# Block 0 of a decoder trunk: query, key, gate and pool columns by seven block products, with the memory's values folded into their weights afterwards

## The chip, the core and the metric

The kernel runs on one core of a Trainium2 chip. The metric is the time on the device for one launch, in microseconds (us). The engines of the core work side by side and wait for each other on semaphores: PE (TensorE) multiplies, ACT (ScalarE) and DVE (VectorE) work on rows of 128 partitions, POOL (GpSimd) here mostly issues DMAs, and SP (SyncE) issues most of the others. DMA moves data between the device memory and the core's own memory.

## What is computed

The reference is one layer of a decoder for 2048 tokens of width 1024, with a memory of 256 tokens, all in fp32. Cut to what matters here:

```python
def reference(x, mem, positions, ...):
    mem_n = rmsnorm(mem, mem_norm_g)
    h = rmsnorm(x, mix_norm_g)
    q, k, v, g, u = split(h @ w_in)            # five column groups of 512
    y_ret  = silu(g) * head_rmsnorm(retention(q, k, v, positions))   # rotary on q and k, 4 heads
    y_pool = pool_mixer(u, pool_w, pool_scale)                       # windows 2, 4, 8, 16
    x = x + concat(y_ret, y_pool) @ w_out
    x = x + cross_attn(rmsnorm(x, xa_norm_g), mem_n, wq, wkv, wo)    # 4 heads of 256
    x = x + conv_glu_ffn(rmsnorm(x, ffn_norm_g), w_up, conv_w, conv_b, w_down)
    return rmsnorm(x, final_norm_g)
```

## The kernel before

**Arithmetic.** Every fp32 operand of a large product is split into a high and a low part (`split`, L254: ACT writes the high part, DVE the low one), and a product is three matmuls that accumulate in one PSUM bank: high by high, high by low, low by high (`passes`, lines L269 to L271). A unit of 128 output columns by 512 tokens over the depth of 1024 is 8 depth tiles by 3, so 24 matmuls of 512 columns. PSUM has five banks for such units (`mm`) and three for small work (`aux`).

**Blocks.** The 2048 tokens are worked in two blocks of 1024. Block 0 runs through the projections, the retention and pooling heads, the output projection and the cross attention; then block 1 does the same; the feed-forward part and the last norm come behind both.

**Seven products.** Block 1 multiplies in the way of Strassen and Winograd. The 16 column groups of 128 of query, key, gate and pool are taken as eight pairs (`PAIRS`, L34). A pair, with the two halves of the depth and the two halves of the tokens, is a two by two block matrix, and its product needs seven block products in place of eight; each is 12 matmuls of 512 columns. For that, sums of quarters of the tokens are made on ACT and DVE (`quarter_sums`, L1603), sums of quarters of the weights by DMAs that add, issued on POOL, into the device tensor `Ad` (`weight_sums`, L1012), and products are added up in SBUF by `head_projections` (L1639). That function also applies the norm and the rotary tables, and starts `retention` (L784) for each head when its parts are there. The feed-forward part uses the same scheme.

**Block 0 before.** Block 0 uses eight products. `head_inputs` (L750) makes gate, query and key of one head as three groups of 48 matmuls, and `pool_group` (L690) the pool columns. The retention of the head before runs between the matmuls as a generator (`behind`), stepped as units go by.

**Folding.** The keys and values of the memory are known before any token arrives, so products of weights that only meet the memory are made once. `folded_weights` (L423) projects keys and values (`project`, 16 steps n of 24 matmuls of 256 columns each), folds the keys into the query weights (M, kept in the device tensor `Md`, 192 matmuls of 256 columns), the values into the output weights of the attention (VW, `VWd`, 96 matmuls of 512 columns), and the pool weights into the output projection (WP, `WPd`, 24 of 512 columns). It is a generator too. The main loop steps it with `folded(n)`: the 16 projection steps stand alone ahead of block 0, and M, VW and WP are taken in small portions between the groups of `head_inputs`. The list `per` says after which group how many portions come.

**Norms.** The squares of the block's tokens are made from the transposed tokens `xT`: ACT squares a tile (`squares_wide` and `load_x`), DVE adds tiles up, and PE sums over the partitions by small matmuls with a column of ones (`stats`), and spreads the factor over the partitions by matmuls with a matrix of ones (`spread`).

**Order.** Instructions of one engine run in the order in which the scheduler puts them, which mostly is the order of the code. A few are pinned (`keep_in_program_order`, `issue_after`). Loads go through SP's queue in order, results are stored through ACT's queue, and the sums of weights go through POOL's software queue; `under` is the generator of the sums, paced by `spacing` and `paced`. Raw weights have five places of 128x1024 in SBUF (`R`, `S`), pairs of split weights three (`Q`); the arenas `B`, `Z` and `TT` hold the rest.

## Time and profile before

| | us |
|---|---|
| runs shown | 2429.25, 2429.44, 2431.54 |
| median | 2429.44 |
| the profiled execution's own time (its span, first to last instruction) | 2429.8 |
| PE busy | 2412.5 (99%) |
| DVE busy | 1722.6 (71%) |
| ACT busy | 1292.3 (53%) |
| POOL busy | 306.1 (13%) |

The profile is of one execution, whose span is 0.36 us above the median. Matmuls overlap each other, so the mean duration of one in a group (some 390 ns) is no price. The price is the distance from start to start, which a full stretch of the view of windows gives as its length by its count. The same holds in a lesser degree for ACT, where a stretch of instructions with no gap between them gives the price of one.

By the trace, the K and V projections of the memory and the loading of block 0 take the first 60 us, with the M, VW and WP portions following among block 0's groups; the stores of VW are issued at 237 to 271 us. POOL's first round of weight sums is issued at 318.9 us. Block 1's values begin at some 650 us and its projections by seven products run to some 960 us.

### The profile page before, as it was taken

How to read it: one execution, taken by the hardware profiler on the slowest of the kernel's cores; microseconds unless marked ns; L12 is line 12 of the kernel's file. 1: busy time of each engine (PE TensorE's matmuls, PEld its weight loads, DVE VectorE, ACT ScalarE, POOL GpSimd, SP SyncE). 2: the span in 40 equal slices, each digit the busy share in tenths (PEclk: the TensorE clock that was granted, in tenths of full speed). 3: DMA queues.
4: the chain of work that ended last, by engine and by line, in shares of the span. 5: the costliest groups of instructions: out<-in, count | busy, mean ns of one | idle time of the engine just before them, and what ended most of it. 6: DMA issues, size and time to landing. Idle time of an engine off the chain costs nothing.

```text
span 2429.8 us, 33360 instructions
## 1 busy us (share of the span) xinstructions
PE 2412.5 (99%) x11328; PEld 2018.4 (83%) x11328; DVE 1722.6 (71%) x2911; ACT 1292.3 (53%) x2360; POOL 306.1 (13%) x477
## 2 busy tenths in 40 slices
PE   9999999999999999999999999999999999999998
PEld 8888888888888888888888888888888888888887
DVE  7756566655857775565788776887677698867875
ACT  6434423444545553334655555765555577666663
POOL 0000012154032444300001010020000000000000
PEclk9999999999999999999999999999999999999999
DMA  7233548699678899985568564755556479758951
GB/s 283 76 105 115 163 137 225 189 237 329 203 206 216 197 254 305 258 293 168 173 223 272 170 204 143 249 191 164 173 158 211 126 244 311 238 183 279 348 178 73
DMA packets 263627, 502.35 MB, mean 207 GB/s; under 512 B 28832, under 2 KB 58016, under 8 KB 263456
## 3 DMA queue, kind: packets, MB, share of 16 engines
q1 hardware_dynamic: 201424, 385.78, 48.3%
q0 software_dynamic: 37376, 86.00, 15.3%
q10 hardware_dynamic: 24656, 28.43, 3.4%
q8 instruction: 89, 1.46, 0.2%
q14 instruction: 82, 0.67, 0.1%
HBM read 398.65 MB, written 187.43 MB: 241 GB/s over the span
## 4 chain that ended last, share of the span: by engine, by line
PE 98%; DVE 1%; ACT 1%; DMA 0%; issue 0%; SPq 0%; DVEq 0%; ACTq 0%
PE mm L269 31%; PE mm L271 30%; PE mm L270 30%; PE aux L269 1%; PE aux L270 1%; PE aux L271 1%; PE aux L832 1%; PE aux L816 1%; PE aux L957 1%; PE aux L805 1%; PE aux L834 1%; DVE Z L241 0%; PE aux L350 0%; PE aux L807 0%; DMA R<-wkv 0%; PE aux L857 0%
## 5 line engine op out<-in xcount | busy, mean ns | idle before, releaser
L269 PE MATMUL mm<-G,Q 128*128 128x512 f32 (+1 forms) x1703 | 656.1, 386 | 3.8 <-ACT Q L257 2.5
L271 PE MATMUL mm<-G,Q 128*128 128x512 f32 (+1 forms) x1703 | 652.9, 384 | 1.4 <-DVE Q L241 1.4
L270 PE MATMUL mm<-G,Q 128*128 128x512 f32 (+1 forms) x1575 | 605.2, 384 | 0.4 <-DVE G L249 0.3
L270 PE MATMUL mm<-G,E 128*128 128x512 f32 x1084 | 421.5, 389 | 0.0
L269 PE MATMUL mm<-G,E 128*128 128x512 f32 x1084 | 420.0, 389 | 0.0
L271 PE MATMUL mm<-G,E 128*128 128x512 f32 x1084 | 419.3, 389 | 0.0
L269 PEld LDWEIGHTS mm<-G,Q 128*128 128x128 f32 x1703 | 320.1, 188 | 67.6 <-ACT Q L257 3.4
L271 PEld LDWEIGHTS mm<-G,Q 128*128 128x128 f32 x1703 | 320.1, 188 | 64.5 <-DVE Q L241 2.0
L270 PEld LDWEIGHTS mm<-G,Q 128*128 128x128 f32 x1575 | 296.0, 188 | 57.3 <-DVE G L249 0.8
L241 DVE TENSOR_TENSOR Z<-Z,mm 128x512 f32<-128x512 f32 (+1 forms) x310 | 207.6, 674 | 121.5 <-PE mm L271 115.7
L249 DVE SCALAR_TENSOR_TENSOR Z<-Z,vecs 128x1024 f32<-128x1024 f32 x176 | 224.8, 1281 | 50.2 <-ACT Z L1191 47.9
L271 PEld LDWEIGHTS mm<-G,E 128*128 128x128 f32 x1084 | 203.5, 188 | 42.4
L270 PEld LDWEIGHTS mm<-G,E 128*128 128x128 f32 x1084 | 203.6, 188 | 42.2
L269 PEld LDWEIGHTS mm<-G,E 128*128 128x128 f32 x1084 | 203.5, 188 | 42.1
L1128 ACT ACTIVATE E<-R 128x512 fp32r<-128x512 f32 (+1 forms) x165 | 101.4, 615 | 144.2 <-PE mm L270 138.3
L241 DVE TENSOR_TENSOR Q<-R,Q 128x512 fp32r<-128x512 f32 x158 | 108.1, 688 | 73.2 <-ACT Q L257 56.0
L241 DVE TENSOR_TENSOR T<-T 128x512 f32<-128x512 f32 (+3 forms) x202 | 138.6, 690 | 21.1 <-ACT T L416 12.1
L241 DVE TENSOR_TENSOR G<-T,G 128x512 fp32r<-128x512 f32 (+1 forms) x185 | 121.6, 677 | 26.5 <-ACT G L1075 13.5
L1075 ACT ACTIVATE G<-T 128x512 fp32r<-128x512 f32 x186 | 112.0, 623 | 32.4 <-DMA T<-Gd 25.7
L1191 ACT ACTIVATE Z<-Z,vecs 128x1024 f32<-128x1024 f32 x88 | 109.1, 1241 | 31.2 <-DVE Z L241 30.2
L1128 ACT ACTIVATE E<-S 128x512 fp32r<-128x512 f32 (+1 forms) x107 | 65.9, 616 | 108.6 <-PE mm L270 106.5
L241 DVE TENSOR_TENSOR E<-R,E 128x512 fp32r<-128x512 f32 (+1 forms) x129 | 86.6, 673 | 44.6 <-ACT E L1128 42.7
(356 smaller groups left out, 3838.2 us busy)
## 6 DMA issues: line engine op xcount, KB each, us to landing
T<-Gd SPq DMA_DIRECT2D x173, 256.0 KB, 4.5
Ud<-w_up POOLq DMA_DIRECT2D x132, 256.0 KB, 9.3
Gd<-Z SPq DMA_DIRECT2D x110, 256.0 KB, 2.8
R<-Ud SPq DMA_DIRECT2D x106, 256.0 KB, 2.7
R<-w_up SPq DMA_DIRECT2D x80, 256.0 KB, 3.1
S<-Ud SPq DMA_DIRECT2D x70, 256.0 KB, 2.8
Gd<-T SPq DMA_DIRECT2D x56, 256.0 KB, 3.4
S<-w_up SPq DMA_DIRECT2D x52, 256.0 KB, 3.2
```

The lines of the kernel that those rows point to most:

```text
L241: return eng.tensor_tensor(out=out, in0=a, in1=b, op=op)
L249: return dve.scalar_tensor_tensor(out=out, in0=a, scalar=s, in1=b, op0=op0, op1=op1)
L269: pe.matmul(ps, lh, rh, start=start, stop=False, skip_group_check=more)
L270: pe.matmul(ps, lh, rl, start=False, stop=False, skip_group_check=more)
L271: latest[0] = pe.matmul(ps, ll, rh, start=False, stop=stop, skip_group_check=more)
L805: pe.matmul(col(sc, c), self.ch(k, c), self.ch(q, c), start=True, stop=True)
L816: pe.matmul(col(self.kv, c), col(self.kn.f, c), self.ch(v, c, h * T), start=True, stop=True)
L832: pe.matmul(col(y, c), col(self.pr.f, c), self.ch(v, c, h * T), start=True, stop=self.cur[c] is None)
L834: pe.matmul(col(y, c), self.ch(q, c), self.cur[c], start=False, stop=True)
L1075: one = act.activation(hi, x, AF.Copy, scale=-1.0 if i == 2 else 1.0)
L1128: act.activation(p2[:, 0, :w], self.raw[i].f[:, :w], AF.Copy)
L1191: act.activation(self.c[g].f, a[:, 2:], AF.Identity, bias=cb[:, f : f + 1], scale=cw[2][:, f : f + 1])
```

## The change

Block 0 now runs through the same functions as block 1: `quarter_sums`, `values` with work between its units, `head_projections` with seven products. `head_inputs`, `pool_group` and `rope_scale` are gone, and `retention` keeps only the form that block 1 used.

What comes with it:

- **The fold is in another place.** M follows the 16 projection steps at once and stands ahead of block 0's values. The projected values of the memory are copied unsplit to a new device tensor `Vd`, since their place in SBUF is wanted for something else, and are read back and split behind block 0's projections. There WP comes first and then VW, all 120 matmuls of 512 columns in one stretch, ahead of the output projection.
- **The weight sums start early.** `weight_sums` is stepped from step n = 17 on and then between the units of the values. `Ad` is read twice, once in each block.
- **Norms come from token rows.** A new input `xR` holds the tokens untransposed. Each of the 16 tiles of 128 tokens is loaded (512 KB) and squared by one ACT instruction that also sums along the row (`token_squares`). The factor is then turned into a row by one small transpose on PE, and spread over the partitions by a store of the row and a load that repeats it (`spread_steps`). The tiles of block 0 are loaded in the 16 projection steps, one a step for the first eight; those of block 1 in the stretch of VW and WP. The squares and sums of `load_x` and `squares_wide` are gone.
- **Rope tables** of block 0 go through the device tensor `rope_d`, as block 1's do.
- Block 1's last half no longer makes the state that nobody reads.

Counted over the whole program, PE has 122 matmuls and transposes fewer: 96 of 512 columns in block 0's projections (672 in place of 768), 8 of 512 columns that spread norms, and 18 small ones (16 of one column and 4 of 128 columns fewer, 2 small transposes more). Matmuls of 256 columns stay at 576. ACT has 128 instructions more, among them the 16 token squares, 22 more high parts of Q and 32 scaled copies of 128 columns; DVE has 39 fewer. SP has 77 DMAs more, 16 of them token tiles of 512 KB. POOL has as many as before.

The main loop, cut:

```diff
-    for n in range(1, 2 * KT):
-        if n in (2, 4, 5, 7, 8, 10, 11, 13):
-            load_x_wide((2, 4, 5, 7, 8, 10, 11, 13).index(n), room)
...
-        if n in (12, 14):
-            wv.append(value_weights(len(wv)))
+    under[0], spacing[0] = weight_sums(), 1
+    xs_at = {KT: 0, KT + 1: 1, KT + 3: 2, KT + 4: 3, KT + 6: 4, KT + 7: 5, 2 * KT: 6, 2 * KT + 1: 7}
+    for n in range(1, 2 * KT + HEADS):
+        if n <= KT:
+            load_tokens(0, n - 1, room)
+        if 1 < n <= KT + 1:
+            token_squares(0, n - 2, room, token_sums)
...
+        if n >= 2 * KT:
+            wv.append(value_weights(n - 2 * KT, B.arenas[(n - 2 * KT) // 2]))
+        if n > 2 * KT:
+            next(under[0])
         folded(1)
...
-            for h in range(HEADS):
-                qkg = head_inputs(h, rb, cs, lambda i: folded(per[h][i]))
-                mix.append(B.take(2))
-                behind[0] = retention(b, h, qkg, v, mix[h])
-            folded(100)
-            slow[0], paced[0], spacing[0] = False, True, 7
-            pooled = {g: pool_group(b, g, rb) for g in (0, 3, 2, 1)}
+        heads = head_projections(b, v, normed[1] if b else rb, t1, t2, z, got)
+        def between():
+            next(behind[0], None)
+            place[0] += 1
+            if b == 0 and place[0] % 2:
+                next(under[0])
...
+            slow[0], paced[0], spacing[0] = False, True, 7
+            for _ in heads:
+                pass
+            room = [Z.take() for _ in range(KT)]
+            for k in range(KT):
+                load_tokens(1, k, room)
+            folded(1)
             for h in range(HEADS):
+                for k in (2 * h, 2 * h + 1):
+                    token_squares(1, k, room, token_sums[:, KT:])
+                folded(1)
```

In the fold, the values take the way over the device memory, and WP comes ahead of VW:

```diff
             if n % 2:
-                for at in (n - 1, n):
-                    split(ps.pop(0), vp4[:, at, 0], vp4[:, at, 1])
+                del ps[:]
+                t = TT.take()
+                act.activation(t.f[:, :SUB], bank[0], AF.Copy)
+                act.dma_start(Vd[n // 2], t.f[:, :SUB])
+                t.free()
...
+        for n in range(0, KT // 2, 2):
+            raw = new_raw()
+            sp.dma_start(raw.rearrange("p (n c) -> p n c", n=2), Vd[n : n + 2].rearrange("n p c -> p n c"))
+            to = vp4[:, 2 * n : 2 * n + 4]
+            split(raw.rearrange("p (n c) -> p n c", n=4), to[:, :, 0], to[:, :, 1])
```

The norms:

```diff
-    def squares_wide(k, room):
+        room[k].free()
+
+    def token_squares(b, k, room, ss):
         f = room[k].f
-        tc.keep_in_program_order(act.activation(f, f, AF.Square))
-        if k:
-            tc.keep_in_program_order(tt(dve, room[0].f, room[0].f, f, ALU.add))
-            room[k].free()
+        tc.keep_in_program_order(act.activation(f, f, AF.Square, accum_out=ss[:, k : k + 1]))
+
+    def load_tokens(b, k, room):
+        tc.keep_in_program_order(sp.dma_start(room[k].f, xR[b * T + k * P : b * T + (k + 1) * P, :]))
```

Three places show how the order moves. The first is SP's queue in the opening, before: tiles of `wkv` (the weights of the memory's keys and values) and of `xT`.

```order
L340 DMA R<-wkv 128x1024
L497 DMA consts<-consts 128x671
L600 DMA Z_74<-xT 128x1024
L340 DMA R<-wkv 128x1024
L340 DMA S_78<-wkv 128x1024
L600 DMA Z_74<-xT 128x1024
L340 DMA S_79<-wkv 128x1024
L600 DMA Z_74<-xT 128x1024
```

The same place after the change, the first token rows `xR` among the same weights.

```order
L353 DMA R<-wkv 128x1024
L510 DMA consts<-consts 128x671
L626 DMA Z_74<-xR 128x1024 x2
L353 DMA R<-wkv 128x1024
L626 DMA Z_74<-xR 128x1024
L353 DMA S_78<-wkv 128x1024
L626 DMA Z_74<-xR 128x1024
L353 DMA S_79<-wkv 128x1024
```

One token tile now stands with each weight tile, and the first `xT` tile comes 14 rows later than before, among the weights of the memory's values.

The second place is PE in block 0's projections, before: the end of a group of `head_inputs` (mm_1094) and the first of M's portions (mm_1161, 256 columns).

```order
L270 MATMUL mm_1094<-G,Q 128x512
L271 MATMUL mm_1094<-G,Q 128x512
L269 MATMUL mm_1161<-G 128x256
L270 MATMUL mm_1161<-G 128x256
L271 MATMUL mm_1161<-G 128x256
```

PE after the change, at the end of block 0's last product (mm_2949), where WP begins (mm_3080 and mm_3086), with the last head's scores (aux_2932) among it.

```order
L273 MATMUL mm_2949<-G,S_1288 128x512
L271 MATMUL mm_3080<-Q 128x512
L272 MATMUL mm_3080<-Q 128x512
L271 MATMUL mm_3086<-Q 128x512
L272 MATMUL mm_3086<-Q 128x512
L273 MATMUL mm_3080<-Q 128x512
L273 MATMUL mm_3086<-Q 128x512
L765 MATMUL aux_2932<-T,Z_74 128x128
```

Portions of the fold that stood between products of block 0 now stand in one row behind them.

The third place is ACT in the fold of the values, before: copies of VW out of PSUM (L552), splits of weights (L257), stores.

```order
L552 ACTIVATE T<-mm_2057,rnm 128x512
L488 DMA VWd<-T 128x4x128
L257 ACTIVATE G<-R 128x512 x4
L552 ACTIVATE T<-mm_2103,rnm 128x512
L488 DMA VWd<-T 128x4x128
L552 ACTIVATE T<-mm_2112,rnm 128x512
L257 ACTIVATE G<-S_78 128x512
```

ACT there after the change, with the squares of block 1's tokens (L622); L591 is VW's copy and L259 the split.

```order
L591 ACTIVATE T<-mm_3209,rnm 128x512
L259 ACTIVATE G<-S_79 128x512
L501 DMA WPd<-T 128x4x128
L501 DMA VWd<-T 128x4x128
L622 ACTIVATE Z_74,halo<-Z_74 128x1024 x2
L591 ACTIVATE T<-mm_3227,rnm 128x512
L501 DMA VWd<-T 128x4x128
L259 ACTIVATE G<-S_3062 128x512
L259 ACTIVATE Q<-S_3062 128x512
L591 ACTIVATE T<-mm_3257,rnm 128x512
```

Squares of 1024 columns, two at a time, now stand ahead of copies that empty PSUM banks.

421 lines of the change are left out of this document (157 added, 264 removed).

## The prediction

> **What bounds the kernel now.** I read the profile's page first, for the shares of the engines and the chain of work that ended last.
>
> ```profile
> span 2429.8 us, 33360 instructions
> PE 2412.5 (99%) x11328; PEld 2018.4 (83%) x11328; DVE 1722.6 (71%) x2911; ACT 1292.3 (53%) x2360; POOL 306.1 (13%) x477
> PE 98%; DVE 1%; ACT 1%; DMA 0%; issue 0%; SPq 0%; DVEq 0%; ACTq 0%
> ```
>
> The chain is PE for 98% of the span. A matmul taken away is therefore worth its full price as long as nobody else becomes late. The price and the places where PE waits come from the view of windows: length, then busy time and count of each engine, then the granted clock, the DMA share and GB/s.
>
> ```profile
> core 0: us, PE busy (x) PEld busy (x) DVE busy (x) ACT busy (x) POOL busy (x), PEclk, DMA share, GB/s
> 0.00:20.00 20.00, 16.77 (x105) 14.97 (x106) 12.99 (x29) 13.99 (x24) 0.20 (x4) 1.00 0.91 341
> 20.00:40.00 20.00, 20.00 (x169) 20.00 (x168) 17.76 (x41) 14.02 (x25) 0.00 (x0) 1.00 0.90 353
> 40.00:60.00 20.00, 17.86 (x124) 16.97 (x123) 16.86 (x29) 13.14 (x25) 0.00 (x0) 0.91 0.49 159
> 126.00:318.00 192.00, 192.00 (x1060) 166.64 (x1059) 116.83 (x246) 76.81 (x177) 0.00 (x0) 1.00 0.41 126
> 1300.00:1400.00 100.00, 100.00 (x443) 82.84 (x442) 79.70 (x104) 55.90 (x83) 9.29 (x11) 1.00 0.67 217
> ```
>
> In 1300 to 1400 us PE has no gap and does 443 matmuls, all but a few of 512 columns, so one costs 100/443 = 0.2257 us. In 20 to 40 us the 169 of 256 columns give 20/169 = 0.118 us. The opening is the one place where PE stands: 3.2 us in the first window and 2.1 us in the third. There the DMA share is 0.9, and ACT and DVE are busy for two thirds and more. The view of waits, cut to PE, names who came last over the whole program.
>
> ```profile
> PE mm L269 <- ACT Q L257: 2.5, 3, 1.8
> PE mm L271 <- DVE Q L241: 1.4, 3, 1.0
> PE aux L805 <- DVE E L249: 1.1, 1, 1.1
> ```
>
> All of that is a few us. So the kernel has little to lose to waits now, and a change can only add to them.
>
> **What is removed.** PE loses 104 matmuls of 512 columns: 104 x 0.2257 = 23.5 us. It loses 18 small ones, net, of one and of 128 columns, for which I take the price of 256 columns as the upper bound: at most 18 x 0.118 = 2.1 us, and at least nothing if they overlap others; I take 2.0, since the row nearest in size is the 256 one. Together 25.5 us, or 1.05% of the span. All of it was on the path, since PE had no gaps in block 0's projections (192.00 us busy of 192). The Trainium skill, "TensorE: Matmul & The Clock Gate", section "Back-to-back issue gap", gives 215.7 ns from start to start for 512 columns, by which the 104 would be worth 22.4 us (an estimate from that page); the trace has 225.7 ns and decides.
>
> **What is added, and what it lies beside.** Four places matter: the opening, M's stretch, the passage from values to seven products, and the stretch of WP and VW. The rows for their ACT and DMA prices:
>
> ```profile
> 61.11 1.16 ACT L257 ACTIVATE G<-S 128x512 fp32r<-128x512 f32 x2 [1.25 <-PE mm L270]
> 65.93 6.73 ACT L606 ACTIVATE Z<-Z 128x1024 f32<-128x1024 f32 x7
> 86.19 2.43 ACT L745 ACTIVATE Z<-mm,rn 128x512 f32<-128x512 f32 x4 [11.28 <-DVE rn L1927]
> L534 ACT ACTIVATE T<-mm,vecs 128x256 f32<-128x256 f32 x32 | 13.3, 470 | 6.9 <-PE mm L271 5.2 <-PE aux L857 1.4 <-ACT G L257 0.3
> L260 ACT ACTIVATE G<-Z,vecs 128x1024 fp32r<-128x1024 f32 x8 | 9.1, 1141 | 0.1
> q0 software_dynamic: 37376, 86.00, 15.3%
> Ad<-w_qkgu POOLq DMA_DIRECT2D x48, 256.0 KB, 9.6
> Ad<-Ad POOLq DMA_DIRECT2D x16, 256.0 KB, 7.6
> ```
>
> Back to back on ACT, a split half costs 1.16/2 = 0.58 us, a square of 1024 columns 6.73/7 = 0.96 us, a scaled copy of 512 columns from PSUM 2.43/4 = 0.61 us. A scaled copy of 256 columns lasts 0.47 us and a wide split of a token tile 1.14 us.
>
> *Opening (16 projection steps).* PE's work is the same, 384 matmuls of 256 columns, 45 us. SP's queue gets eight token tiles of 512 KB and the `xT` tiles later. At the 353 GB/s of the second window, 512 KB take 1.5 us, so a step's weight and token tile take 3.0 us where PE's 24 matmuls take 2.8 us. That is even, so loads keep up or lag by 0.2 us a step, 1 to 2 us over eight steps. Later the wkv tiles come with `xT` tiles, as before. In the other direction, fewer wide splits stand on ACT and DVE in the first half, which may take away some of the 2.1 us in the third window. I take 0, with -4 (most of the present waits go) to +4.
>
> *M's stretch.* 192 matmuls of 256 columns, 22.7 us of PE, formerly spread among groups of block 0 where ACT had time. ACT's work there: 16 split halves of `wqT`, 9.3 us; 32 scaled copies, 15.0 us; 8 split halves of the value weights, 4.6 us; two wide splits of `xT`, 2.3 us. That is 31.2 us. The value weights' splits can lag into the values, and some splits can be done ahead, as far as five raw places allow. Without the first and with two steps ahead I come to some 4 us late. Bounds: 0 (all is made ahead) and 8.5 (31.2 less 22.7).
>
> *From values to products, and the products.* Block 1 runs the same code in the trace of before:
>
> ```profile
> 700.00:840.00 140.00, 140.00 (x734) 119.37 (x733) 99.09 (x203) 71.34 (x173) 49.44 (x79) 1.00 0.81 209
> 840.00:860.00 20.00, 18.17 (x94) 15.17 (x93) 17.40 (x36) 14.84 (x31) 12.74 (x20) 1.00 1.08 260
> 860.00:960.00 100.00, 99.45 (x468) 82.70 (x468) 60.21 (x110) 40.22 (x94) 43.27 (x69) 1.00 1.00 278
> ```
>
> In 140 us of it PE has no gap, with DVE at 71% and ACT at 51%, so the splitting of operands and adding of products are hidden. The loss is 1.8 and 0.6 us where it passes to the last heads. Block 0 will pay the same: +2.4 us, bounds 0 and 5. Rope tables and quarter sums lie beside the 192 matmuls of the values, 43 us; the quarter sums did so in block 1 without a gap.
>
> *WP and VW in one stretch.* Before, the VW fold stood in two portions of two heads each, with a head's group between them:
>
> ```profile
> 240.00:250.00 10.00, 10.00 (x48) 8.26 (x47) 7.16 (x14) 8.09 (x14) 0.00 (x0) 1.00 0.75 208
> 250.00:260.00 10.00, 10.00 (x46) 8.29 (x45) 5.99 (x10) 2.15 (x4) 0.00 (x0) 1.00 0.66 212
> 260.00:272.00 12.00, 12.00 (x60) 10.12 (x60) 4.95 (x9) 8.25 (x14) 0.00 (x0) 1.00 0.74 213
> ```
>
> ACT was at 81% and 69% in the portions and had a rest of 10 us between; PE lost nothing. Now 120 matmuls stand in one row, 27.1 us. ACT's work beside them: 24 split halves (13.9), 24 scaled copies (14.6), 2 wide splits of the values read back (2.3), 8 token squares of block 1 (7.7): 38.5 us. That is 11.4 us too much for the stretch, of which the first split halves can be made during the last products, where ACT is at 40%, as far as the raw places go (some eight halves, 5 us). I take +6 us, with 2 and 15. The upper end adds 4 us for loads: wo, `wout_p`, `xR` and the values read back come to about 21 tiles of 512 KB, 10.5 MB, 30 us at 353 GB/s for a stretch of 27. PE waits for ACT there since a copy empties the PSUM bank, and behind ACT's squares, which nobody needs yet, the copies and the stores of VW queue.
>
> *The rest.* The seven-product sums for block 0 are made by the same 64 DMAs, only earlier. Norms by token rows take ACT and DVE work off block 1's loading, where PE was not waiting: 0. The output projection of block 0 waits for WP, which is stored first, ahead of 22 us of VW: 0.
>
> **Sum.** 2429.8 - 25.5 + 0 + 4 + 2.4 + 6 = 2416.7 us of span. The median of the runs is 0.4 us below the profiled span, so 2416 us, 0.55% faster. A difference of 0.2% (4.9 us) is about what a measurement of this kernel can tell from no change.
>
> **The clock, a price that may come on top.** These lines of PE's timeline are from the third window:
>
> ```profile
> 39.77 0.28 PE L271 MATMUL mm<-G,Q 128*128 128x256 f32 x1
> 39.90 0.28 PE L269 MATMUL mm<-G,Q 128*128 128x256 f32 x1
> 44.27 0.39 PE L269 MATMUL mm<-G,Q 128*128 128x256 f32 x1 [1.75 <-ACT Q L257]
> 46.71 0.41 PE L271 MATMUL mm<-G 128*128 128x256 f32 x1
> 46.92 0.41 PE L269 MATMUL mm<-G 128*128 128x256 f32 x1
> ```
>
> A wait of 1.75 us was followed by matmuls 0.21 us apart where they had been 0.13 apart, and the window's granted clock is 0.91: 9% of 20 us, 1.8 us lost beside the wait. If the added waits come in pieces as long as that, each brings up to 1.8 us more. I expect pieces under 1 us (a bank that is emptied late), and count nothing. The Trainium skill, same page, section "Part 1: The HAM clock gate", has the clock halve only after an idle window of about 3.4 us; by that rule even pieces of 2 us would be free and the sum stays at 2416, but the trace shows a halved stretch behind a shorter wait, so the rule is not leaned on.
>
> **Rivals.**
>
> *Everything is hidden.* ACT makes splits far enough ahead in M's stretch and in WP and VW, and the opening loses no more than now. For it: PE lost nothing in the portions at 240 and 260 us, at 81% of ACT. Against it: the 38.5 us of work in 27.1. Time: 2429.4 - 25.5 = 2404 us.
>
> *The folds are bound by ACT and the loads, and eat the gain.* M's stretch loses 8, WP and VW 12, the passage 3, and one or two long waits halve the clock: 2429.4 - 25.5 + 23 + 2 = 2429 us, no change. For it: both stretches are over their ACT budget, the opening's DMA is full. Against it: work can be made ahead, and the products before have ACT at half.
>
> *Slower: the weight sums come too late.* In block 0, a pair is 7 x 12 x 0.2257 = 19.0 us of PE, and needs its four sums in `Ad`, each reached through a chain of three DMAs on POOL's queue (9.6, 9.6 and 7.6 us to landing by the rows above). They start about 75 us into the program, and the first pair needs them at about 60 + 23 + 43 = 126 us. It decides where a round of eight DMAs takes longer than 19 us: at 24 us PE would wait 5 us for each of seven pairs, 35 us, and the time is 2416 + 35 = 2451. For it: the queue shares the 16 DMA engines with SP's loads, at their busiest just then. Against it: 86 MB in 15.3% of 2429.8 us is 372 us for about 330 DMAs, 1.1 us of all 16 engines for one and 9 us for a round, less than half of a pair. The Trainium skill, "DMA: Bandwidth & Descriptors", section "Queues, rings and completion order", says that each DMA engine goes round between the queues that have work, a packet from each in turn; so neither queue is shut out, and the sums would slow SP's loads rather than wait for them. No row of before shows the two together at full load.
>
> **How the numbers follow.** My forecast, some waits in both folds and a net gain of 8 to 20 us, has 0.50; its own range is 2409 to 2422. All hidden has 0.20, the gain eaten 0.15, slower by late sums 0.15. That 2416 stands is the likeliest case. The range from the bounds: best, opening -4, M 0, passage 0, WP and VW +2, so 2402; worst without late sums, +4, +8.5, +5 and +15, so 2436. All four at one end together is unlikely, so 2403 to 2433 leaves about 2 in 10 out, most of it above. Faster by over 0.2% (under 2424.6) takes the forecast, all hidden and a small part of the eaten gain: 0.73. Within 0.2% takes most of the rest of the eaten gain: 0.11. Slower takes late sums and a tail: 0.16.
>
> **What would show it.** Right: PE has 122 instructions fewer; the products of block 0 run at 100% PE from some 126 us on with no waits on `Ad`; the waits of PE name ACT (copies out of PSUM, or high parts) in M's stretch at about 60 to 85 us and in WP and VW at about 280 to 320 us, some 4 and 6 us; ACT is near 95% busy there. Wrong step by step: gaps at the opening with loads late (the 0 for the opening); PE waiting on DMAs of `Ad` or on Q split from it (late sums); no gap in either fold (all hidden); pieces of idle time followed by a granted clock under 1 (the price counted at nothing). Wrong altogether: a time above 2433, or a loss in a place not named here, such as the attention or the feed-forward part.

## The result

The changed kernel takes 2470.38 us (median of four runs, 2465.41 to 2471.11) against 2429.9 us (2429.25 to 2431.54): 1.6% slower, ratio 1.016 with a 95% interval of 1.0146 to 1.0174. The forecast was 2416 us and a range that ended at 2433. The profiled execution has a span of 2468.2 us against 2429.8, so 38.4 us more.

From the page of the changed kernel: span, busy time, the slices of PE and of its granted clock, and the chain.

```profile
span 2468.2 us, 33388 instructions
...
PE 2403.8 (97%) x11186; PEld 2002.1 (81%) x11186; DVE 1717.3 (70%) x2872; ACT 1355.2 (55%) x2498; POOL 308.2 (12%) x477
...
PE   9779999999999999999999999999999999999998
...
PEclk9889998999999999999999999999999999999999
...
PE 83%; DVE 1%; ACT 0%; issue 0%; DVEq 0%; ACTq 0%
```

PE and its granted clock drop in the second and third of the 40 slices of 62 us, and the clock again in the seventh. From the eighth on the two kernels look alike (before, every slice of PE but the last reads 9, and every slice of the clock), so nearly all of the loss lies in the first 430 us. The chain was followed back only to 395.7 us, by its first piece: 84% of the span, nearly all of it PE's, and it says nothing of the part before that. PE's busy 2403.8 us, only 8.7 fewer than before, mislead: matmuls at half clock count as busy.

The view of windows shows where.

```profile
60.00:80.00 20.00, 15.18 (x117) 14.12 (x116) 11.49 (x17) 15.44 (x34) 7.26 (x12) 1.00 0.94 340
80.00:100.00 20.00, 8.16 (x40) 7.19 (x39) 3.79 (x6) 6.23 (x15) 5.22 (x8) 0.68 0.96 288
...
120.00:140.00 20.00, 20.00 (x90) 16.57 (x89) 13.49 (x23) 7.00 (x15) 11.22 (x17) 1.00 0.84 227
140.00:160.00 20.00, 8.96 (x35) 6.54 (x33) 17.49 (x31) 12.76 (x23) 6.45 (x11) 0.80 0.81 193
160.00:180.00 20.00, 13.53 (x36) 10.39 (x37) 4.58 (x8) 2.92 (x7) 10.52 (x18) 0.69 1.09 312
...
360.00:380.00 20.00, 12.58 (x41) 8.25 (x40) 17.14 (x41) 15.86 (x35) 0.00 (x0) 0.67 0.94 328
```

PE stands in three places: in M's stretch (60 to 100 us), at the start of block 0's products (140 to 180 us), and in the stretch of WP and VW (360 to 380 us). In each the granted clock falls too, and in each the DMA share is 0.8 to 1.1. At 80 to 100 us ACT and DVE are busy for only 6.23 and 3.79 of 20 us, so it isn't the amount of their work that holds PE there. The view of waits names who came last.

```profile
PE mm L271 <- ACT G L259: 20.3, 5, 11.8
PE mm L271 <- ACT Q L1636: 10.4, 2, 9.9
PE mm L271 <- ACT S L1636: 6.4, 1, 6.4
PE mm L271 <- ACT T L571: 3.5, 2, 2.9
```

ACT is named each time, since it makes the high parts. What ACT itself waited for stands in its own rows, from 60 to 180 us. "issue" is time in which it waited for nothing that this view names.

```profile
ACT S L1636 <- DMA S<-w_qkgu: 15.4, 1, 15.4
...
ACT T L548 <- issue: 9.0, 1, 9.0
```

And the queue that issues those loads, SP's, in the same stretch:

```profile
SPq L1903 <- ACT T L681: 18.2, 1, 18.2
...
SPq L1508 <- DMA Md<-T: 15.5, 2, 8.1
```

At the start of the products ACT stood 15.4 us for a raw weight block of 256 KB. In M's stretch it stood 9.0 us, and its timeline shows where:

```profile
78.55 1.21 ACT L548 ACTIVATE T<-mm,vecs 128x256 f32<-128x256 f32 x3
87.68 0.93 ACTq L501 DMA_DIRECT2D Md<-T  x2
88.72 1.21 ACT L548 ACTIVATE T<-mm,vecs 128x256 f32<-128x256 f32 x3 [8.96 <-issue]
```

Between two groups of M's copies (L548) stand stores of M, which ACT issues in its own order. As far as the semaphores in the trace tell, the first of them waited for a store of M that had been issued at 66.9 us and landed at 87.6. So the longest wait of M's stretch, 11.8 us of PE, comes from M's stores: its last weights were issued at 72.3 us and had landed at 84.5.

SP's queue stood 18.2 us at the store of the rope tables (L1903), with the first products' weights queued behind it. DVE, which makes these tables, had itself stood behind a store of M, up to 110.7 us:

```profile
DVE T L247 <- DMA Md<-T: 14.8, 1, 14.8
```

One view across both kernels tells most of it: the first 100 us and the next 60, of before and then of after.

```profile
0.00:100.00 100.00, 94.63 (x589) 85.77 (x590) 72.15 (x143) 58.88 (x97) 0.20 (x4) 0.98 0.55 197
100.00:160.00 60.00, 60.00 (x318) 51.79 (x317) 41.24 (x65) 25.29 (x46) 0.00 (x0) 1.00 0.40 123
```

```profile
0.00:100.00 100.00, 78.29 (x570) 74.02 (x571) 61.03 (x125) 68.76 (x133) 12.69 (x24) 0.94 0.95 343
100.00:160.00 60.00, 48.97 (x228) 40.37 (x227) 36.91 (x63) 26.13 (x51) 23.44 (x37) 0.93 0.90 232
```

Before, the 16 DMA engines were busy for 55 + 24 = 79 us of the first 160. Now they are busy for 95 + 54 = 149. (A share can pass 1, as the 1.09 above, so it measures crowding and not work alone.) The changed kernel needs a good deal of that ahead of its first product, which by PE's work alone would have begun at some 126 us.

To put a number on each place I took the starts of all matmuls in a trace and added up what each step exceeds the usual distance for its width (0.2266, 0.119 and 0.111 us for 512, 256 and fewer columns), so that waits and halved clock are both in. Only steps that exceed it by more than 0.05 us count, each where it ends. The sums, in us:

| kernel | 0 to 60 | 60 to 100 | 100 to 200 | 300 to 400 | elsewhere | all |
|---|---|---|---|---|---|---|
| before | 10.9 | 0.1 | 0.8 | 0.7 | 13.6 | 26.1 |
| after | 9.0 | 20.8 | 24.6 | 21.4 | 16.1 | 91.9 |
| e1, sums later | 8.9 | 4.8 | 15.0 | 23.4 | 15.2 | 67.3 |
| e2, rope stores on ACT | 8.5 | 19.2 | 21.0 | 22.1 | 18.9 | 89.7 |
| e4, no sums | 9.1 | 6.1 | 5.7 | 21.3 | 14.2 | 56.4 |
| e6, e1 paced, tokens late | 9.0 | 4.8 | 13.6 | 18.7 | 14.8 | 60.9 |
| e8, before with early sums | 10.7 | 0.1 | 0.8 | 0.7 | 14.5 | 26.7 |
| g2, e6 with WP early | 8.8 | 10.6 | 16.1 | 10.3 | 14.0 | 59.8 |
| h1, g2 without sums | 8.7 | 10.9 | 10.5 | 10.6 | 16.4 | 57.0 |

The span less the last column is PE's own work: 2403.7 us before and 2376.3 after. PE did save its matmuls, 27.4 us. It then lost 65.8 us more to waits, and 65.8 - 27.4 = 38.4 us is the difference of the spans.

### The profile page after: what moved, and what is told of

It is laid out like the page before. It is cut to its first block, busy times and chain, and to the rows that moved or that the text cites. A ratio compares the mean times of both kernels' runs of the same rounds, so it can differ in the third digit from the quotient of the medians.

```text
span 2468.2 us, 33388 instructions
## 1 busy us (share of the span) xinstructions
PE 2403.8 (97%) x11186; PEld 2002.1 (81%) x11186; DVE 1717.3 (70%) x2872; ACT 1355.2 (55%) x2498; POOL 308.2 (12%) x477
## 3 DMA queue, kind: packets, MB, share of 16 engines
q0 software_dynamic: 37376, 86.00, 14.9%
## 4 chain that ended last, share of the span: by engine, by line
PE 83%; DVE 1%; ACT 0%; issue 0%; DVEq 0%; ACTq 0%
PE mm L271 26%; PE mm L272 26%; PE mm L273 26%; PE aux L271 1%; PE aux L273 1%; PE aux L272 1%; PE aux L855 1%; DVE Z L243 0%; PE aux L363 0%; PE aux L765 0%; PE aux L763 0%; PE aux L735 0%; PE aux L747 0%; PE aux L778 0%; PE aux L737 0%; DVE T L243 0%
## 5 line engine op out<-in xcount | busy, mean ns | idle before, releaser
L271 PE MATMUL mm<-G,Q 128*128 128x512 f32 (+1 forms) x1665 | 642.1, 386 | 19.1 <-ACT Q L1636 10.4
L273 PE MATMUL mm<-G,Q 128*128 128x512 f32 (+1 forms) x1665 | 637.7, 385 | 2.3 <-DVE Q L243 2.3
L272 PE MATMUL mm<-G,Q 128*128 128x512 f32 (+1 forms) x1537 | 590.4, 384 | 0.4 <-DVE G L251 0.2
L272 PE MATMUL mm<-G,E 128*128 128x512 f32 (+1 forms) x1092 | 420.4, 385 | 0.0
L271 PE MATMUL mm<-G,E 128*128 128x512 f32 (+1 forms) x1092 | 418.8, 385 | 0.7 <-ACT E L259 0.7
L273 PE MATMUL mm<-G,E 128*128 128x512 f32 (+1 forms) x1092 | 418.3, 385 | 0.2 <-DVE E L243 0.2
L271 PEld LDWEIGHTS mm<-G,Q 128*128 128x128 f32 x1665 | 315.2, 189 | 84.0 <-ACT Q L1636 11.6
L273 PEld LDWEIGHTS mm<-G,Q 128*128 128x128 f32 x1665 | 314.8, 189 | 64.5 <-DVE Q L243 3.8
L272 PEld LDWEIGHTS mm<-G,Q 128*128 128x128 f32 x1537 | 291.1, 189 | 56.3 <-DVE G L243 1.2
L243 DVE TENSOR_TENSOR Z<-Z,mm 128x512 f32<-128x512 f32 (+1 forms) x322 | 215.0, 671 | 124.2 <-PE mm L273 122.7
L243 DVE TENSOR_TENSOR Q<-R,Q 128x512 fp32r<-128x512 f32 x180 | 122.5, 686 | 83.3 <-ACT Q L259 53.7
L243 DVE TENSOR_TENSOR T<-T 128x512 f32<-128x512 f32 (+4 forms) x196 | 134.1, 688 | 24.8 <-ACT T L432 12.4
L243 DVE TENSOR_TENSOR G<-T,G 128x512 fp32r<-128x512 f32 (+1 forms) x169 | 110.3, 672 | 38.4 <-ACT G L259 18.7
```

The lines of the kernel that those rows point to most:

```text
L243: return eng.tensor_tensor(out=out, in0=a, in1=b, op=op)
L271: pe.matmul(ps, lh, rh, start=start, stop=False, skip_group_check=more)
L272: pe.matmul(ps, lh, rl, start=False, stop=False, skip_group_check=more)
L273: latest[0] = pe.matmul(ps, ll, rh, start=False, stop=stop, skip_group_check=more)
```

## The experiments

Names in the theories: A, the sums of weights and the loads share the DMA engines, so loads that PE needs at once come late; B, SP's queue stands behind the rope store; C, ACT has too much work (the forecast's reason for both folds); D to H as they come. All times of before below are from the same chip as the kernel they stand beside. The kernels ran on several chips, where the median of before was 2429.9 to 2431.84 us, so a difference of 1 or 2 us between two changed kernels says little.

### When the sums of weights run

e1 starts them with the values in place of beside M:

```diff
-        if n > 2 * KT:
-            next(under[0])
         folded(1)
```

> Weight sums of block 0 start with the values in place of M's stretch; nothing else is changed. Theory A (the sums on POOL's queue and SP's loads share the DMA engines, and M waits for its weights): the waits of 16.5 us at 60 to 100 us and the halved clock behind them go, the sums run denser beside the values and the first pairs may wait longer; 2450 to 2460 us. Rival C (M waits because ACT has too much work there, as I had forecast): the waits stay and the sums come later, 2470 us or more.

2444.51 us against 2431.84, ratio 1.0053 (1.0038 to 1.0068): 26 us better than the changed kernel, and 5.5 us below the range of theory A. M's stretch lost 4.8 us in place of 20.8, with the same work on ACT, which speaks for A there and against C. The start of the products gained too, more than expected.

```profile
60.00:80.00 20.00, 17.51 (x130) 16.81 (x129) 13.67 (x21) 18.35 (x40) 0.00 (x0) 0.91 0.96 351
80.00:100.00 20.00, 20.00 (x115) 17.57 (x114) 6.78 (x13) 10.45 (x25) 2.58 (x6) 1.00 0.82 281
...
140.00:160.00 20.00, 12.81 (x48) 10.04 (x47) 7.65 (x14) 3.40 (x8) 9.47 (x16) 0.83 1.05 323
```

From 80 to 100 us PE has no gap now. From 140 to 160 us it still does, with POOL busy, ACT and DVE mostly idle and a DMA share of 1.05: the sums stand beside the first products instead. And what the changed kernel doesn't have appears here: SP's queue waits for the sums themselves, 16.2 us between 60 and 320 us (9.1 on `Ad<-Ad` and 7.1 on `Ad<-w_qkgu`).

e2 leaves the sums and takes the rope stores off SP's queue:

```diff
-            sp.dma_start(rope_d[b][i], r.f[:, :SUB])
+            (sp if b else act).dma_start(rope_d[b][i], r.f[:, :SUB])
```

> The three stores of block 0's rope tables go through ACT's queue in place of SP's; nothing else is changed. Theory B (SP's queue stands 18 us behind the store that waits for the tables, so the first pair's weights are loaded late): the wait of 9.9 us at 157 us shrinks to 3 us or less, and the one of 6.4 us at 174 us too, since the loads no longer meet the next round of sums; 2455 to 2462 us. Theory A alone: the loads are late in any case because the DMA engines are full, 2467 to 2471 us.

2465.71 us, ratio 1.0138 (1.0121 to 1.0154), some 5 us better, between the two ranges. The wait at the first product did not shrink (11.2 us up to 156 us, on ACT's high part, for 9.9), only the second one did (2.9 for 6.4 us). B alone is refuted as the main reason. With the store gone, SP's queue stood as long at the next load of a sum, 18.9 us behind a step of DVE's, and issued it at 149.0 us for 152.3. DVE had stood 15.6 us behind a store of M here too.

e3 makes both edits.

> Both edits: sums from the values on, rope stores through ACT's queue. If A and B hold side by side, both gains add: 2436 to 2450 us, with what is left in the stretch of WP and VW (some 17 us). If the sums beside the values are what makes the products late, it is no better than with the later sums alone, 2450 to 2460 us.

2445.04 us, ratio 1.0055 (1.004 to 1.007). That lies in the range for gains that add, but e1 alone is as good, so they don't add.

e4 takes the sums' traffic away. It leaves out the sums of w_qkgu, and the products read raw blocks of the same size.

```diff
-                super().__init__([w_qkgu[n] for n in PAIRS[p]], Ad[p], 0, 4)
+                w = [w_qkgu[n] for n in PAIRS[p]]
+                super().__init__(w, [block(w, i // 2, i % 2, 0, 4) for i in range(4)], 0, 4)
```

> The sums of w_qkgu are left out: POOL issues no DMA for them, and the products read raw weight blocks of the same size where they read sums (so the values computed differ). Everything else, the rope stores on SP's queue too, is as in the changed kernel. Theory A: M's waits (16.5 us) and the one at 174 us go with their halved clock, the one at 157 us stays in part; 2438 to 2450 us. If the traffic of the sums does not matter: 2465 to 2471 us.

2434.55 us in one run, 36 us better than the changed kernel and 3 us below the range of theory A. The first 160 us of e4:

```profile
0.00:100.00 100.00, 91.45 (x654) 86.84 (x655) 65.40 (x133) 74.56 (x147) 2.35 (x8) 0.97 0.89 334
100.00:160.00 60.00, 55.95 (x242) 44.59 (x241) 51.41 (x88) 29.01 (x55) 14.28 (x25) 1.00 0.62 187
```

Without the sums, DMA is busy for 89 + 37 = 126 us of 160, and PE's loss falls to 6.1 and 5.7 us in the two places. The stretch of WP and VW is as bad as in the changed kernel, 21.3 us: that loss is another one.

e8 makes the opposite test, the sums alone, in the kernel before:

```diff
+    under[0], spacing[0] = weight_sums(), 1
     for n in range(1, 2 * KT):
+        if 1 < n < 14:
+            next(under[0])
```

> The kernel before, with one part of the change alone: twelve rounds of the sums are issued in the opening, one with each projection step from the third to the fourteenth, where DMA is 0.9 busy and nobody needs them yet. Theory A: loads of the memory's weights land later and PE waits for them; 15 to 35 us slower than before, 2445 to 2465 us. If the loads have way over the sums, or the loss in the changed kernel comes from needing the sums early: 2430 to 2434 us.

2432.29 us in one run against 2431.2: nothing. This was against my own theory, and it is the most useful run of all.

```profile
0.00:100.00 100.00, 94.68 (x590) 85.98 (x591) 70.17 (x140) 58.87 (x108) 39.12 (x70) 0.98 1.01 332
100.00:160.00 60.00, 60.00 (x317) 51.79 (x316) 43.23 (x68) 24.44 (x46) 25.93 (x38) 1.00 1.08 286
```

The DMA engines are as full as in the changed kernel, 1.01 and 1.08, and PE's row is that of before. The first sums went out at 34 us, when the loads of the opening were nearly all issued. What came later was not spared: over the whole run the tiles of `wqT` landed in 7.4 and 9.3 us (median, in `R` and `S`) for 3.6 and 4.1 before, and the stores of M in 5.7 us for 2.2. The tiles land later than in the changed kernel, and PE lost nothing. In this kernel M's portions stand far apart, between groups of block 0, which leaves time for what lands late. Neither full DMA engines nor a late load cost anything by themselves. They cost where a load or a store with no slack is behind other traffic, as M's stores and the loads of the first products were.

### Pacing, and the token tiles of block 1

e5 is e1 with six rounds of sums beside the values in place of eight:

```diff
-            if b == 0 and place[0] % 2:
+            if b == 0 and place[0] in (1, 3, 5, 7, 11, 15):
```

> Sums from the values on as before, but after four rounds only two more follow beside the values (six in place of eight); the rest come one in seven products. Theory A: the wait of 7.2 us at 151 us of the later sums, where the first pair's raw weights land late behind dense rounds, goes to 2 us or less; 2436 to 2441 us. If the sums are then too late for their pair: a wait on a load from Ad in the products, 2445 us or more.

2441.32 us, ratio 1.0043 (1.0028 to 1.0058). The wait at 151 us went from 7.2 to 6.1 us only, so dense rounds were not the point. SP's queue now waited 24.1 us for sums, where e1 had 16.2.

e6 adds to e5 that block 1's token tiles are loaded and squared one a unit beside the output projection:

```diff
-            for k in range(KT):
-                load_tokens(1, k, room)
...
+            if b == 0:
+                load_tokens(1, n, room)
+                if n:
+                    token_squares(1, n - 1, room, token_sums[:, KT:])
```

> As e5, and the eight token tiles of block 1 are loaded and squared beside the output projection of block 0, in place of the stretch of WP and VW. Theory D (that stretch waits for loads and for ACT, and the token tiles are 4 MB of its loads and 8 us of its ACT work): its 18 us of lost time shrink to 6 to 11 us, 2427 to 2434 us. If the stretch waits for the values read back and for the places of the raw weights alone: within 3 us of e5.

2438.48 us, ratio 1.003 (1.0018 to 1.0042); 18.7 us lost at 300 to 400 us where e5 lost 20.9. So 4 MB of loads and 8 us of ACT's work were worth 2 to 3 us, a third of what theory D wanted and within the 3 us of its rival.

e7 is e6 with POOL held back in the last ten products:

```diff
-            next(under[0], None)
+            if b or at < own - 10:
+                next(under[0], None)
```

> As e6, and no round of sums is issued in the last ten products of block 0. Theory E (the reading back of the values takes 7 us beside a round of eight sums, and ACT stands behind it): the wait at the head of the stretch, some 5 us with the halved clock behind it, goes; 4 to 8 us below e6. If ACT's order alone makes it: no change from e6.

2441.17 us, ratio 1.0043 (1.0026 to 1.0059), not better than e6. In its trace the wait at the head of the stretch is shorter (1.0 for 2.7 us), and a later one, on a copy out of PSUM, stays (4.3 for 5.4 us). E is refuted as the reason, though the first wait shrank as it said.

### What holds the stretch of WP and VW

f3 is e5, but loads two tiles of wo once and splits them for all four heads (values differ), so six loads of 512 KB are gone from the stretch and PE, ACT and DVE do the same work:

```diff
+        held = [raw_places().take() for _ in range(2)]
+        for dt in range(2):
+            sp.dma_start(held[dt].f, wo[dt * P : (dt + 1) * P, :])
         for h in range(HEADS):
-            dp = [row_pairs(wo[(2 * h + dt) * P : (2 * h + dt + 1) * P, :]) for dt in range(2)]
+            dp = [pairs(held[dt].f) for dt in range(2)]
```

> As e5, but the two raw tiles of wo are loaded once and split again for each head (six loads of 512 KB fewer in the stretch of WP and VW; the values computed differ), with the same work on PE, ACT and DVE. Theory F: the stretch loses 5 to 10 us less than in e5, 2431 to 2437 us. Rival C (ACT's own work bounds the stretch): within 3 us of e5, 2439 to 2443 us.

2439.92 us, ratio 1.0035 (1.0023 to 1.0047), 1.4 us below e5. Theory F, DMA as the bound of the stretch, fails (the edit also holds two of the five raw places, which may cost something). The windows of f3 there:

```profile
320.00:340.00 20.00, 15.84 (x88) 12.97 (x87) 18.76 (x39) 13.92 (x37) 2.77 (x5) 1.00 0.99 291
340.00:360.00 20.00, 15.55 (x53) 11.71 (x53) 17.11 (x39) 16.07 (x35) 0.00 (x0) 0.66 0.65 190
```

DVE is busy for 18.76 and 17.11 of 20 us where PE loses most, and ACT for 14 and 16. The forecast had counted ACT there and left DVE out, which has the low parts of every split, the last pool columns and the last head at the same time. That DVE is what holds PE is not shown: the longest waits of PE there name ACT (4.2 us on a high part, 4.4 us in two waits for a copy), and no run takes work off DVE alone.

f1 is e6 with the four heads of VW put between units of the output projection; f2 is f1 without sums, f4 is f1 with the rope stores on ACT's queue and with block 0's later sums three times as far apart (`spacing[0]` 21 for 7).

```diff
-            folded(1 + HEADS)
+            folded(1)
...
+            if b == 0 and n % 2 == 0:
+                folded(1)
```

> As e6 (later, paced sums; token tiles of block 1 beside the output projection), and the four heads of VW stand between units of block 0's output projection in place of one stretch ahead of it. Theory F (the stretch of WP and VW is bound by DMA: loads of 15 tiles of 512 KB and stores of 24 of 256 KB, 14 MB in 27 us of PE, where no window moved more than some 400 GB/s): most of the 18 us lost there goes, 2424 to 2431 us. If what is late is the reading back of the values and the first WP weights: only 2 to 4 us better than e6, 2434 to 2437 us.

> The changed kernel without the sums of w_qkgu (POOL issues none of them, the products read raw weight blocks, so the values computed differ), and with VW and the token tiles of block 1 beside the output projection. If the two losses, sums at full DMA and the stretch, make nearly all of what the change cost, they add: 2413 to 2422 us, which is near the forecast that left both out. If something else is late instead: 2428 us or more.

> As f1, with the rope stores through ACT's queue and the sums paced three times slower through block 0's output projection. If the DMA share is what is left to gain there: 2 to 5 us below f1. If the rope stores and late rounds matter no more: within 2 us of f1.

They took 2451.03 us (ratio 1.0083, 1.0069 to 1.0097), 2448.1 us (one run) and 2445.0 us (1.0059, 1.0046 to 1.0073), all worse than e6 or e4. By the code, the edit is at fault: the places lent to VW's split weights, and those of the memory's split values, are those of the tiles that the output projection writes, so VW is made from overwritten values, and one waits for the other. The runs say nothing of the idea.

g1 is e5 without the reading back and splitting of the memory's values, so that VW is made from what lies there.

```diff
-            raw = new_raw()
-            sp.dma_start(raw.rearrange("p (n c) -> p n c", n=2), Vd[n : n + 2].rearrange("n p c -> p n c"))
-            to = vp4[:, 2 * n : 2 * n + 4]
-            split(raw.rearrange("p (n c) -> p n c", n=4), to[:, :, 0], to[:, :, 1])
+            pass
```

> As e5, without reading back and splitting the memory's values (VW is made from what lies in that place, so the values computed differ): two loads of 512 KB, two wide splits on ACT and on DVE fewer. Theory G (ACT stands in its order behind the loads that come late through few places, the reading back first of all): the wait of 5.6 us at the head of the stretch and the halved clock behind it go, 2433 to 2437 us. Otherwise within 2 us of e5.

2437.59 us, ratio 1.0027 (1.0016 to 1.0037): 3.7 us below e5, 0.6 above the range of theory G. The stretch lost 17.4 us for 20.9: part of the wait, not its reason.

g2 puts WP behind M, ahead of the values; all else is e6.

```diff
-    for n in range(1, 2 * KT + HEADS):
+    for n in range(1, 2 * KT + HEADS + 1):
...
-        if n >= 2 * KT:
+        if 2 * KT <= n < 2 * KT + HEADS:
             wv.append(value_weights(n - 2 * KT, B.arenas[(n - 2 * KT) // 2]))
```

> As e6 (later, paced sums; token tiles beside the output projection), and WP stands behind M, ahead of the values, so that only VW and the reading back are left behind the products. Theory G: the first copies and splits of the stretch, which wait for four tiles of WP's weights and two of values at once, are thinned out; 5 to 10 us below e6, 2428 to 2434 us. If the stretch is bound by ACT and DVE throughout, WP's 5.4 us of PE cost as much wait in their new place, where ACT was free: 2 to 4 us below e6.

2446.1 us (2438.01 to 2447.3), ratio 1.0057 (1.0043 to 1.007), far above both ranges. The profiled execution is the fastest of the five, so no trace shows what made the others up to 9 us longer. In its trace the stretch behind the products loses 10.3 us for 18.7, the gain that theory G wanted, and the new place of WP loses 5.8 us more and the start of the products 2.5. The windows of g2:

```profile
80.00:100.00 20.00, 15.72 (x88) 12.44 (x87) 7.92 (x13) 13.94 (x30) 0.00 (x0) 1.00 1.00 352
...
340.00:360.00 20.00, 16.44 (x88) 12.86 (x87) 17.60 (x37) 13.06 (x35) 0.00 (x0) 1.00 0.77 272
```

So the crowd at the head of the stretch is 8.4 of the 18.7 us lost there, and moving a part of it to where DMA is at 1.00 gives as much back: by the profiled executions g2 is 1 us faster than e6.

### What is left at the start of the products

g3 is g2 with e2's edit, the rope stores on ACT's queue.

> As g2, with the rope stores on ACT's queue. Theory B, now without dense sums to hide it: the first pair's weights are loaded some 10 us earlier and the 13 us lost at 120 to 160 us shrink to some 6; 3 to 7 us below g2. If the loads there are late because of the sums alone: within 2 us of g2.

2440.94 us, ratio 1.0045 (1.0032 to 1.0057), below g2's median by 5 us, as theory B had it. Whether B is the reason is open: the trace of g3 is its slowest execution and that of g2 its fastest, and between these two the loss at 100 to 200 us did not shrink (17.3 for 16.1). There SP's queue no longer stood at the rope store (14.8 us in g2), but waited for the sums longer, 18.3 us on `Ad<-Ad` for 7.7 between 60 and 180 us.

g4 is g3 with one round of sums moved from beside the values to ahead of them, and the others one step earlier:

```diff
+        if n == 2 * KT + HEADS:
+            next(under[0])
...
-            if b == 0 and place[0] in (1, 3, 5, 7, 11, 15):
+            if b == 0 and place[0] in (1, 3, 5, 9, 14):
```

> As g3, with the first round of sums beside WP, ahead of the values, and the others one step earlier. If the first pairs' sums are what makes the products late: 1 to 4 us below g3. If it brings the sums back among the loads of M and WP: 2 to 6 us above g3.

2451.54 us, ratio 1.0082 (1.0068 to 1.0096), 11 us above g3 and beyond both ranges. By the profiled executions the start of the products lost 24.4 us for g3's 17.3, and nothing else got worse. So earlier sums cost time, but at the first products and not among the loads of M and WP.

h1 is g2 with e4's edit: no sums, raw blocks read in their place.

> As g2 (WP behind M, token tiles beside the output projection), with the sums of w_qkgu left out: POOL issues none of them and the products read raw weight blocks, so the values computed differ. If the loss is the traffic of the sums ahead of and beside the products plus the crowding of WP and VW, both are gone here and most of the 27 us that PE saves comes out: 2418 to 2426 us, faster than before. If the seven products themselves, or the fold in one piece, are what is slow: 2430 us or more.

2435.62 us (ten runs, 2431.92 to 2441.59), ratio 1.002 (1.001 to 1.0029). The first expectation failed: with the traffic gone and the stretch thinned, it was still no faster than before. Beside e4, which has no sums either, it loses 4.8 us more in each of the first two places and 10.7 us less in the stretch, so moving WP and the token tiles gained nothing in sum. At the start of the products it loses 10.5 us without a single sum.

```profile
140.00:160.00 20.00, 12.77 (x44) 9.49 (x43) 14.07 (x23) 10.25 (x21) 4.85 (x10) 0.74 0.76 222
```

And the longest waits of SP's queue in h1, from 60 to 180 us:

```profile
SPq L1515 <- DVE T L248: 14.2, 1, 14.2
SPq L1911 <- ACT T L683: 13.3, 1, 13.3
```

SP's queue stood 14.2 us behind a step of DVE's, at a load for the quarter sums (L1515), and 13.3 us at the rope store (L1911), one after the other.

h2 is e6 with block 0's rope tables made beside M and the value weights (`rope0`, handed on to the place where they were made).

```diff
+        if n >= 2 * KT:
+            for _ in range(4):
+                next(rope0, None)
```

> As e6, with block 0's rope tables made on DVE and ACT beside M (four steps with each of its last four generator steps) in place of beside the values, and stored through ACT's queue. Theory H (what is left at the start of the products, some 13 us, comes from DVE, which has rope tables and quarter sums to do in the second half of the values, and from SP's queue behind the rope store): the loss there shrinks to 5 us or less, 2428 to 2433 us. If the loads of the first pairs beside the sums make it: within 3 us of e6, 2435 to 2441 us.

2449.15 us, ratio 1.007 (1.0056 to 1.0084), 11 us above e6 and beyond both ranges. In the profiled execution, the slowest of the five, M's stretch lost 14.9 us and the start of the products 14.2. Theory H fails in this form. The work on DVE and ACT beside M delays M, and the start is late all the same. What makes the last 6 to 14 us there is left open; of the things tried, none alone was it. No version tried beats the kernel before.

## Why the prediction was wrong

**The step that failed** is "The seven-product sums for block 0 are made by the same 64 DMAs, only earlier", priced at 0. It is the largest part: without the sums the kernel takes 36 us less (e4, one run), 33.6 of them in M's stretch and at the start of the products. The number to start from is the DMA engines' time ahead of the first product. The rows were there: 0.91, 0.90 and 0.49 of the first three windows of 20 us, 46 us in all, then 64 sums at 1.1 us of all engines, 70 us, and beside them the token tiles, the second reading of `xT`, `wqT` and M's stores. That makes far more than PE's 126 us leave room for without queueing, and 149 us of 160 were measured. The total alone does not decide: e8 has 101 + 65 = 166 us in the same 160 and lost nothing. The second half of the step that failed is that "only earlier" puts the sums beside stores and loads that PE needs within a few us, M's and the first products', where before they ran beside work with slack.

**Its rival had the mechanism in half.** "The weight sums come too late" ended on the right side, 2451 us, but by a wait that hardly occurred. From 100 to 320 us the only wait of ACT for a sum is this one:

```profile
ACT Q L1636 <- DMA R<-Ad: 0.6, 1, 0.6
```

PE and DVE have none, and no wait of SP's queue there is put down to a sum. The longest wait of ACT, 15.4 us, was for a raw block. What happened stood in its last sentences: that the sums would slow other transfers rather than wait for them, argued from the Trainium skill ("DMA: Bandwidth & Descriptors", section "Queues, rings and completion order"), where each DMA engine takes a packet from each queue in turn. The trace agrees in that no engine waited for a sum for more than 0.6 us. What was slowed shows in the DMA issues (times, KB, median us to landing), the stores of M and the tiles of `wqT`, of before,

```profile
Md<-T ACTq DMA_DIRECT2D x16, 256.0 KB, 2.2
...
R<-wqT SPq DMA_DIRECT2D x5, 512.0 KB, 3.6
...
S<-wqT SPq DMA_DIRECT2D x3, 512.0 KB, 4.1
```

of the changed kernel,

```profile
Md<-T ACTq DMA_DIRECT2D x16, 256.0 KB, 7.9
...
R<-wqT SPq DMA_DIRECT2D x5, 512.0 KB, 5.4
...
S<-wqT SPq DMA_DIRECT2D x3, 512.0 KB, 7.3
```

and of e4, without sums:

```profile
Md<-T ACTq DMA_DIRECT2D x16, 256.0 KB, 6.1
...
R<-wqT SPq DMA_DIRECT2D x5, 512.0 KB, 5.3
...
S<-wqT SPq DMA_DIRECT2D x3, 512.0 KB, 6.6
```

Most of the later landing is there without sums, so it comes with the fold in one piece and not with them. What the sums add is in M's stores, 7.9 us for 6.1, and more so in the latest ones: up to 16.1 us where e4 has at most 8.0 (the view of the tile `Md`, which times most of them). At the start of the products three raw blocks landed in 14.9 us (median, 100 to 180 us) where e4 has 6.3. The prediction had drawn no price from it.

**What is removed**: 25.5 us was forecast, 27.4 us measured. Right. The rest is in the small ones: the program has 122 instructions fewer, but the trace has 142 records fewer, since each matmul of one column stands in it as two. Of these 38 are small, and at 0.111 us they make 4.2 us, for the 2.0 of the forecast.

**Opening**: 0 forecast, 1.9 us gained. Right within its bounds.

**M's stretch**: +4 forecast, +6.0 without the sums (e4), +20.7 with them. The term was of the right size, and the sums lay on top. Its reason, too much work for ACT, was not shown: in e1, with the same ACT work and no sums beside M, the loss was 4.8 us, and what makes it was not tried.

**Passage to the products**: +2.4 forecast, +4.9 without the sums, +23.8 with them. That block 1 runs the same code almost without loss was no evidence for block 0: by the code, block 1 has its sums and its rope tables ready before its values begin. The products themselves ran as forecast once they had begun, here in e4:

```profile
160.00:300.00 140.00, 140.00 (x732) 119.36 (x731) 97.95 (x207) 71.33 (x170) 40.86 (x63) 1.00 0.73 191
```

**WP and VW**: +6 forecast, bounds 2 and 15, +20.7 measured. The place was right, and the term was sized too small, beyond its upper bound. DVE was not counted, and the clock was counted at nothing. Of what else fills it, the runs show parts alone: 8.4 us go when WP stands elsewhere (g2), 3.5 when the values are not read back (g1), about 1 when six loads are gone (f3). The rest stays open.

**The clock**: "I expect pieces under 1 us, and count nothing." The waits came in pieces of 2 to 12 us, and the clock fell in four of the six windows above, to 0.67 to 0.80. Steps of up to about double the usual distance make some 13 of the 66.8 us lost in the three places.

With the terms as measured and no sums, 2429.8 - 27.4 - 1.8 + 6.0 + 4.9 + 20.6 + 0.6 elsewhere = 2432.7 us, the span of e4 (2432.8). Even then the change would have gained nothing: the two stretches of folding (26.6 us) took what the products gave.

## What to carry to other kernels

When a change moves traffic to an earlier stage, add up the DMA engines' busy time that must be over before a given matmul, as you would for PE, from the shares in the windows and the price of one transfer; an average share over the program says nothing of it. Then ask which loads and stores in that time have slack. Full DMA engines cost nothing where nothing near them is urgent (e8), and 7 to 16 us a place where the next load or store has no slack (g4 against g3, M's stretch in the changed kernel against e1). Look at stores as well as loads: an engine that issues them in its own order can stand behind one, as ACT did for 9.0 us. Work that was spread among matmuls as filler has a price when it is gathered in one stretch, and every engine that touches it has to be counted there, not only the one that looks busiest in the average.

## What the runs showed of the hardware that was not expected

Some of the changed kernels scatter more than the kernel before. Thirteen runs of before beside h1 lie within 3.7 us (2428.99 to 2432.7); ten of h1 lie within 9.7 us and five of g2 within 9.3 us. Four of e1 lie within 2.9 us, so not all do. What makes the scatter was not tried.

The clock's price has a tail. These are rows of PE's timeline in the changed kernel, start first:

```profile
94.48 0.58 PE L271 MATMUL mm<-G 128*128 128x256 f32 x1 [11.84 <-ACT G L259]
...
95.93 0.41 PE L271 MATMUL mm<-G 128*128 128x256 f32 x1
96.14 0.41 PE L272 MATMUL mm<-G 128*128 128x256 f32 x1
...
98.92 0.63 PE L271 MATMUL mm<-G 128*128 128x512 f32 x1
99.34 0.63 PE L272 MATMUL mm<-G 128*128 128x512 f32 x1
...
100.88 0.39 PE L273 MATMUL mm<-G 128*128 128x512 f32 x1
101.11 0.39 PE L271 MATMUL mm<-E,G 128*128 128x512 f32 x1
```

Behind the wait of 11.84 us the matmuls of 256 columns start 0.21 us apart, not 0.12, and those of 512 columns 0.42 us apart, not 0.23, until some 100.6 us: six microseconds of matmuls at half rate, which cost three more beside the wait.
